# No Pool work in layer 0's projections, and the first 512 scales' weights between the two halves of the tokens

## The chip, the cores and the metric

The kernel runs on one core of a Trainium2 chip. The metric is the time of one execution on the device in microseconds (us), the median of three runs. In the profile the engines are PE (matrix products; PEld is its loading of weights), DVE (vector), ACT (scalar), POOL (general) and SP, which here only issues loads. ACT issues the stores of layer 0's projections.

## What is computed

Two layers of a diffusion backbone over 1024 tokens of 2048 channels in float32, with a context of 256 tokens. Layer 0 is attention, layer 1 a pooling layer. What matters here is how layer 0 begins: a modulation vector made from a conditioning vector scales and shifts the normed tokens, and the result is multiplied with a wide matrix.

```python
def _modulation(cvec, w, b):
    m = jax.nn.silu(cvec) @ w + b
    m = m[..., None, :]
    return m[..., :D_MODEL], m[..., D_MODEL:2 * D_MODEL], m[..., 2 * D_MODEL:]
...
    shift, scale, gate = _modulation(c, mod_w, mod_b)
    shift_c, scale_c, gate_c = _modulation(c_ctx, mod_w, mod_b)
    h = _rmsnorm(x, pre_g) * (1 + scale) + shift
    hc = _rmsnorm(ctx, pre_g) * (1 + scale_c) + shift_c

    proj = h @ w_in
    qA, qB = _split_q(proj[..., :Q_W])
    kA, vA, kB, vB = _split_kv(proj[..., Q_W:Q_W + KV_W])
    z = proj[..., Q_W + KV_W:]
...
    qA = _rope(_rmsnorm(qA, q_norm), cos, sin)
    kA = _rope(_rmsnorm(kA, k_norm), cos, sin)
```

Queries and keys get a rotary turn, the queries of 16 heads and the keys and values of 4 go to scratch in DRAM, and the gates `z` follow. Attention, the output projection and layer 1 come after that and are not touched.

## The kernel before

**Products.** Each float32 operand of a large product is cut into a high and a low part (`split`, line 144): ACT (or Pool) writes the rounded high part, DVE (or Pool) writes the source less the high part. A product is three passes, high by high, high by low, low by high. A 128x512 matmul is the unit of work of PE: three column blocks of 128, two halves of 512 tokens, 16 chunks of 128 rows and three passes make 288 of them. Weights come through tiles `wr` (two buffers) and are split into `wh` (ACT) and `wl` (DVE).

**Modulation.** `modulation(kind, j)` makes 512 channels of the scales (`kind` 1) or shifts (`kind` 0). It loads eight tiles `mraw` of 512 KB, two chunks of 128 rows each, through five buffers (`RAWS`), multiplies each of the 16 chunks by a column of the conditioning vector and adds the products up. `mod_add` (line 341) does a chunk on DVE (accumulator `mac`, line 355) or, for the chunks in `SHARED`, on ACT (`mpr`, line 349) and Pool (accumulator `max`, line 350). Of the scales' chunks Pool adds 9 of 16 (6 of the first 512 channels), of the shifts' 6. `mod_columns` (line 359) sums both accumulators over the partitions on PE (tile `mc`), and `mod_set` puts the result into `s0` or `b0`.

**The start.** `tokens(n)` loads a half of the tokens as four tiles `x` of 1 MB, takes their mean squares on ACT (line 396), and scales them on Pool and DVE in turn (line 398). `turned(n, ...)` transposes them on PE (`tx`, line 407), and ACT and DVE copy the result into `xT`.

**First two products.** `first` makes three blocks of queries with `hs`, which is `xT` times the scale without the shift (`scaled`: the high part on ACT, line 458, the low part on DVE, line 459). It goes by quarters of four chunks: quarter j needs `modulation(1, j)`. `second` makes three further blocks with the full `h` (`modulated`: `nw` on ACT, high part on Pool, low part on DVE); quarter j needs `modulation(0, j)`. What the missing shifts add to `first` is made later (`first_shifts`).

**The other blocks.** `step` makes two blocks at a time (192 matmuls) and then does some tasks of the rest of the modulation (`mod_rest`, all on DVE). Each query head's half goes through `q_out`: a copy `hc` and squares `sq` on ACT, the rotary turn (`rotated`: three operations on DVE into `ra` and `rt`, one buffer each, and a sum on Pool, line 537), a split into `hl` (high on ACT, low on Pool) and two stores. PE sums the squares over the partitions (`cs`, line 549).

**What sets the order.** A scheduler puts the instructions of each engine into one fixed order, and each engine runs its list strictly in that order. A load that waits for a free buffer holds up all later loads of the same queue.

```python
            if k in shared:
...
                    nc.scalar.activation(pr, w, AF.Copy, scale=c)
                    nc.gpsimd.tensor_tensor(accs[1], accs[1], pr, op=ALU.add)
...
                nc.vector.scalar_tensor_tensor(accs[0], w, c, accs[0], op0=ALU.mult, op1=ALU.add)
```

Of the kernel before, what the change touches and what calls it, by code (L numbers as in the profile page):

```python
# [17 lines left out]
P = 128  # L18
D = 2048
# [11 lines left out]
# A product of two float32 numbers, each cut exactly into two 12-bit parts.  # L31
PASSES = ((0, 0), (0, 1), (1, 0))
WT, WB, PB = 512, 4, 8
RAWS = 5
# [13 lines left out]
# Chunks of rows whose products ACT and Pool take, for shifts and scales.  # L48
SHARED = (1, 4, 7, 9, 12, 15), (1, 3, 5, 7, 9, 11, 13, 14, 15)


def _constants():
# [7 lines left out]
    # Blocks of keys before, at and after the queries' own; the context's are all open.  # L60
# [18 lines left out]
def tile_backbone(ctx, tc, ins, out):  # L79
# [4 lines left out]
    # Sums of the modulation over the rows, still to be added up over the partitions.  # L84
# [19 lines left out]
    # Which of four lots of partitions a partition belongs to.  # L104
# [24 lines left out]
    # Scratch in DRAM.  # L129
# [23 lines left out]
    def w_tiles(w, cols, kc=KC, hi="act", room=None):  # L153
        """Chunks of 128 rows of the weights w, in two parts: the first chunk, their number and the tiles."""
# [36 lines left out]
    def newton(r, v, t):  # L191
        """r = 1 / sqrt(v), with a Newton step; t is room for it."""
        nc.scalar.activation(r, v, AF.Sqrt)
        nc.vector.reciprocal(r, r)
        nc.vector.tensor_tensor(t, r, r, op=ALU.mult)
        nc.vector.tensor_tensor(t, t, v, op=ALU.mult)
        nc.vector.tensor_scalar(t, t, -0.5, 1.5, op0=ALU.mult, op1=ALU.add)
        nc.vector.tensor_tensor(r, r, t, op=ALU.mult)

    def rstd_rows(r, ss, tp, n, tag):  # L200
        """r = 1 / sqrt(ss / D + eps), elementwise."""
# [4 lines left out]
    def lots_of(d, a):  # L206
        """512 columns of d, as lots of 32 partitions with 128 columns of four of d's rows each."""
# [10 lines left out]
    # ---------------------------------------------------------------- attention weights  # L218
# [3 lines left out]
    # The pools of the units with an even number and, later, those with an odd one.  # L222
# [14 lines left out]
    def scores(u, kt, s_tile, c_tile, pinned=lambda i: i, pin=lambda i: i, band=None):  # L237
        """Attention weights of four heads' blocks of queries, with queries on the partitions."""
# [53 lines left out]
    # ---------------------------------------------------------------- layer 0: norms and projections  # L292
    with ExitStack() as st:
# [13 lines left out]
        # Small vectors, one column per 128 channels.  # L307
# [15 lines left out]
        # Scales and shifts of the attention layer's tokens, 512 channels at a time: products with the rows of the  # L323
        # weights, which the partitions add up first.
# [16 lines left out]
        def mod_add(accs, k, w, c, tp, shared):  # L341
            """Adds a chunk's products, on DVE or, the shared ones, on ACT and Pool."""
            if k in shared:
                if accs[1] is None:
                    accs[1] = tp.tile([P, 512], F32, tag="max", name="max", bufs=2)
                    nc.scalar.activation(accs[1], w, AF.Copy, scale=c)
                else:
                    pr = tp.tile([P, 512], F32, tag="mpr", name="mpr", bufs=2)
                    nc.scalar.activation(pr, w, AF.Copy, scale=c)
                    nc.gpsimd.tensor_tensor(accs[1], accs[1], pr, op=ALU.add)  # L350
            elif accs[0] is None:
                accs[0] = tp.tile([P, 512], F32, tag="mac", name="mac", bufs=2)[:, : w.shape[1]]
                nc.vector.tensor_scalar(accs[0], w, c, None, op0=ALU.mult)
            else:
                nc.vector.scalar_tensor_tensor(accs[0], w, c, accs[0], op0=ALU.mult, op1=ALU.add)  # L355

        def mod_columns(accs, n=4):
            """The sums over the partitions, a column per 128 channels."""
            t = mtile("mc")
            accs = [a for a in accs if a is not None]  # L360
            for i in range(n):
                for a in accs:
                    nc.tensor.matmul(t[:, i : i + 1], lhsT=a[:, i * P : (i + 1) * P], rhs=ones[:, 0:1], start=a is accs[0], stop=a is accs[-1])
# [13 lines left out]
        def modulation(kind, j, shared=None):  # L377
            accs = [None, None]
            for k, w in mod_rows("ev", kind, j, raws):
                mod_add(accs, k, w, csil[:, k, 0:1], p0, shared or SHARED[kind])  # L380
            with tc.high_priority(offset=AHEAD):
                mod_set(kind, j, 0, mod_columns(accs))

        # Tokens scaled by their root mean squares, then with channels on the partitions.
# [5 lines left out]
        def tokens(n):  # L390
            xt = []
            for t in range(4 * n, 4 * n + 4):
# [5 lines left out]
                (nc.vector if t % 2 else nc.gpsimd).tensor_scalar(a, a, rx[:, t : t + 1], 1.0, op0=ALU.mult, op1=ALU.mult)  # L398
# [18 lines left out]
        def project(c0, nm, beside=None):  # L417
            """Products of blocks c0.. of w_in's columns with the tokens, by (block, half), with others between them."""
# [15 lines left out]
        def three(c0):  # L434
            """Three blocks, by halves, and the weights' tiles, two chunks of rows at a time."""
# [743 lines left out]
```

## Time and profile before

| what | value |
|---|---|
| time, median of 3 runs | 3113.48 us (3112.36 to 3114.37) |
| the profiled execution | span 3115.6 us; no other time is recorded for it |
| PE busy | 2989.6 us, 96% |
| DVE busy | 1649.9 us, 53% |
| ACT busy | 1075.0 us, 35% |
| POOL busy | 424.1 us, 14% |
| mean granted clock of PE | 0.981 of full speed |

The busy shares are means over stages that differ. The start, `first` and `second` fill the first 239 us, the query steps go to about 560 us, gates, keys and values to about 1105 us, the last gates and attention to 1607 us, and the rest is the output projection and layer 1. A granted clock of 1.00 is PE's level of 2.4 GHz; at 0.5, 1.2 GHz, a matmul takes twice as long. A stretch with a clock of 0.87 is one in which PE ran part of the time at half speed.

### The profile page before, as it was taken

How to read it: one execution, taken by the hardware profiler on the slowest of the kernel's cores; microseconds unless marked ns; L12 is line 12 of the kernel's file. 1: busy time of each engine (PE TensorE's matmuls, PEld its weight loads, DVE VectorE, ACT ScalarE, POOL GpSimd, SP SyncE). 2: the span in 40 equal slices, each digit the busy share in tenths (PEclk: the TensorE clock that was granted, in tenths of full speed). 3: DMA queues.
4: the chain of work that ended last, by engine and by line, in shares of the span. 5: the costliest groups of instructions: out<-in, count | busy, mean ns of one | idle time of the engine just before them, and what ended most of it. 6: DMA issues, size and time to landing. Idle time of an engine off the chain costs nothing.

```text
span 3115.6 us, 38559 instructions
## 1 busy us (share of the span) xinstructions
PE 2989.6 (96%) x14102; PEld 2481.0 (80%) x14102; DVE 1649.9 (53%) x2725; ACT 1075.0 (35%) x2073; POOL 424.1 (14%) x327
## 2 busy tenths in 40 slices
PE   5899999899999999999899999999999999999998
PEld 5677777787888788888778888888888888888887
DVE  7968877555235748888753363623332323322434
ACT  6542312221111147776642352522222221222332
POOL 4643413000001100001220040300000001000000
PEclk8989999999999999999999999999999999999999
DMA  8738776888467854445555544423222121355734
GB/s 289 242 126 252 215 247 219 254 289 260 171 235 253 267 177 124 136 125 159 153 170 164 214 138 157 156 65 111 85 91 75 48 101 49 129 176 172 250 104 163
DMA packets 373011, 530.34 MB, mean 170 GB/s; under 512 B 28644, under 2 KB 215894, under 8 KB 371670
## 3 DMA queue, kind: packets, MB, share of 16 engines
q1 hardware_dynamic: 287990, 445.81, 44.7%
q10 hardware_dynamic: 84832, 82.07, 7.7%
q8 instruction: 111, 1.82, 0.2%
q14 instruction: 78, 0.64, 0.1%
HBM read 428.88 MB, written 98.91 MB: 169 GB/s over the span
## 4 chain that ended last, share of the span: by engine, by line
PE 70%; DMA 13%; DVE 9%; issue 3%; ACT 2%; POOL 2%; SPq 0%; ACTq 0%; DVEq 0%; POOLq 0%
PE g L186 32%; PE g L962 21%; DMA mraw<-in_od_mod_w_dram 5%; DVE mac L355 5%; PE o L904 4%; DMA mraw<-in_ev_mod_w_dram 3%; PE mx L186 3%; PE s L254 3%; PE t L850 3%; PE g L1043 2%; DVE wl L149 1%; DMA lsd<-ls 1%; DMA wr<-in_od_w_out_dram 1%; DMA rs<-lsd 1%; PE c L260 1%
## 5 line engine op out<-in xcount | busy, mean ns | idle before, releaser
L149 DVE TENSOR_TENSOR wl<-wr,wh 128x512 fp32r<-128x512 f32 (+1 forms) x576 | 414.9, 726 | 852.6 <-ACT wh L146 835.4
L186 PE MATMUL g<-h,wh 128*128 128x512 f32 x2368 | 756.8, 400 | 8.1 <-ACT fe L477 5.8
L146 ACT CAST wh<-wr 128x512 fp32r<-128x512 f32 (+1 forms) x576 | 349.6, 615 | 1100.2 <-PE g L186 563.5
L962 PE MATMUL g<-wh,a 128*128 128x512 f32 x1920 | 594.4, 390 | 0.1
L186 PE MATMUL g<-a,wh 128*128 128x512 f32 x1856 | 571.0, 389 | 0.0
L186 PEld LDWEIGHTS g<-h,wh 128*128 128x128 f32 x2368 | 453.9, 194 | 100.7 <-POOL h L148 5.9
L186 PE MATMUL g<-h,wl 128*128 128x512 f32 x1184 | 473.9, 401 | 14.2 <-DVE wl L149 14.1
L355 DVE SCALAR_TENSOR_TENSOR mac<-mraw,csil,mac 128x512 f32<-128x512 f32 x423 | 364.5, 862 | 120.2 <-DMA mraw<-in_od_mod_w_dram 64.8
L962 PEld LDWEIGHTS g<-wh,a 128*128 128x128 f32 x1920 | 360.1, 188 | 75.5 <-ACT wh L146 0.8
L186 PEld LDWEIGHTS g<-a,wh 128*128 128x128 f32 x1856 | 348.3, 188 | 72.4
L962 PE MATMUL g<-wl,a 128*128 128x512 f32 x960 | 373.7, 389 | 0.0
L186 PE MATMUL g<-a,wl 128*128 128x512 f32 x928 | 360.7, 389 | 0.0
L186 PEld LDWEIGHTS g<-h,wl 128*128 128x128 f32 x1184 | 227.9, 193 | 67.0 <-DVE wl L149 19.9
L962 PEld LDWEIGHTS g<-wl,a 128*128 128x128 f32 x960 | 180.2, 188 | 37.2
L186 PEld LDWEIGHTS g<-a,wl 128*128 128x128 f32 x928 | 174.2, 188 | 36.3
L149 DVE TENSOR_TENSOR tl<-t,th 128x512 fp32r<-128x512 f32 x236 | 160.0, 684 | 39.5 <-ACT th L146 38.0
L146 ACT CAST th<-t 128x512 fp32r<-128x512 f32 x236 | 135.9, 584 | 110.6 <-PE t L850 109.3
L904 PE MATMUL o<-th,vt 128*128 128x512 f32 x472 | 156.3, 412 | 2.5 <-ACT th L146 2.5
L850 PE MATMUL t<-ident,p 128*128 128x128 f32 x944 | 139.0, 276 | 10.5 <-DVE tl L149 10.1
L850 PEld LDWEIGHTS t<-ident,p 128*128 128x128 f32 x944 | 114.8, 142 | 38.2 <-DVE tl L149 15.5
L537 POOL TENSOR_TENSOR ra<-ra,rt 128x512 f32<-128x512 f32 x40 | 64.7, 1619 | 553.1 <-DMA mraw<-in_ev_mod_w_dram 287.8
L1106 POOL TENSOR_TENSOR s<-s 128x541 f32<-128x541 f32 (+1 forms) x32 | 38.1, 1190 | 587.4 <-DVE s L1106 561.7
(221 smaller groups left out, 3357.2 us busy)
## 6 DMA issues: line engine op xcount, KB each, us to landing
mraw<-in_ev_mod_w_dram SPq DMA_DIRECT2D x192, 256.0 KB, 4.0
mraw<-in_od_mod_w_dram SPq DMA_DIRECT2D x192, 256.0 KB, 4.6
wr<-in_od_w_in_dram SPq DMA_DIRECT2D x76, 512.0 KB, 3.6
wr<-in_ev_w_in_dram SPq DMA_DIRECT2D x68, 512.0 KB, 4.6
mraw<-in_ev_mod_w_dram SPq DMA_DIRECT2D x64, 512.0 KB, 5.2
wr<-in_ev_w_out_dram SPq DMA_DIRECT2D x64, 512.0 KB, 3.8
wr<-in_od_w_out_dram SPq DMA_DIRECT2D x64, 512.0 KB, 4.8
qd<-hl ACTq DMA_DIRECT2D x64, 256.0 KB, 2.9
```

What stands on the lines that cost most here:

```text
L146: nc.scalar.copy(dst_h, src)
L149: (lo or nc.vector).tensor_tensor(dst_l, src, f32(dst_h), op=ALU.subtract)
L186: pin(nc.tensor.matmul(o, lhsT=w[a][:, kk, m * P : (m + 1) * P], rhs=rhs(n, k, b), start=(k == 0 and i == 0), stop=(k == kc - 1 and i == 2),))
L254: pin(nc.tensor.matmul(s[:, sl], lhsT=qt[:, h, a], rhs=kt[:, b, sl], start=i == 0, stop=i == 2))
L260: pinned(nc.tensor.matmul(cs[:, hh], lhsT=qt[:, h + hh, a], rhs=kt[:, b, L:], start=i == 0, stop=i == 2))
L355: nc.vector.scalar_tensor_tensor(accs[0], w, c, accs[0], op0=ALU.mult, op1=ALU.add)
L537: nc.gpsimd.tensor_tensor(a, a, t, op=ALU.add)
L850: pin(nc.tensor.transpose(t[:, h * P : (h + 1) * P], ps[h][:, i * P : (i + 1) * P], ident))
L904: pin(nc.tensor.matmul(outs[u], lhsT=vt[:, a, kb], rhs=b, start=(i == 0 and jj == 0), stop=(last and jj == 2)))
L962: nc.tensor.matmul(o, lhsT=y[k][:, a, t * P : (t + 1) * P], rhs=wt[b][:, k - k0, :], start=(k == 0 and i == 0), stop=(k == KC - 1 and i == 2),
L1043: mm = nc.tensor.matmul(o, lhsT=w[a][:, k - k0, m * P : (m + 1) * P], rhs=hT[k][0][:, b], start=(k == 0 and i == 0), stop=(k == KC - 1 and ...
L1106: eng.tensor_tensor(nx[:, lo + d :], cur[:, lo + d :], cur[:, lo : W - d], op=ALU.add)
```

## The change

Pool is taken out of layer 0's projections, and the order of the start is changed:

- All 16 chunks of a modulation are multiplied and added on DVE; `SHARED`, `max` and `mpr` are gone, and `mod_columns` sums one accumulator.
- `mraw` has seven buffers in place of five.
- Every second tile `x` is scaled on ACT in place of Pool.
- The high part of `h`, and that of the context's tokens, is made on ACT in place of Pool.
- The sum of the rotary turn and the low part of `hl` (queries and keys) are made on DVE in place of Pool.
- The first half of the tokens is loaded and turned, then comes `modulation(1, 0)`, then the second half. Before, both halves came first.

Lines that were only comments are blank in the changed file, and its line numbers are up to ten lower.

```diff
-RAWS = 5
+RAWS = 7
...
-        def mod_add(accs, k, w, c, tp, shared):
-            """Adds a chunk's products, on DVE or, the shared ones, on ACT and Pool."""
-            if k in shared:
-                if accs[1] is None:
-                    accs[1] = tp.tile([P, 512], F32, tag="max", name="max", bufs=2)
-                    nc.scalar.activation(accs[1], w, AF.Copy, scale=c)
-                else:
-                    pr = tp.tile([P, 512], F32, tag="mpr", name="mpr", bufs=2)
-                    nc.scalar.activation(pr, w, AF.Copy, scale=c)
-                    nc.gpsimd.tensor_tensor(accs[1], accs[1], pr, op=ALU.add)
-            elif accs[0] is None:
-                accs[0] = tp.tile([P, 512], F32, tag="mac", name="mac", bufs=2)[:, : w.shape[1]]
-                nc.vector.tensor_scalar(accs[0], w, c, None, op0=ALU.mult)
+        def mod_add(a, k, w, c, tp):
+
+            if a is None:
+                a = tp.tile([P, 512], F32, tag="mac", name="mac", bufs=2)[:, : w.shape[1]]
+                nc.vector.tensor_scalar(a, w, c, None, op0=ALU.mult)
             else:
-                nc.vector.scalar_tensor_tensor(accs[0], w, c, accs[0], op0=ALU.mult, op1=ALU.add)
...
+                nc.vector.scalar_tensor_tensor(a, w, c, a, op0=ALU.mult, op1=ALU.add)
+            return a
...
-                (nc.vector if t % 2 else nc.gpsimd).tensor_scalar(a, a, rx[:, t : t + 1], 1.0, op0=ALU.mult, op1=ALU.mult)
+                if t % 2:
+                    nc.vector.tensor_scalar(a, a, rx[:, t : t + 1], 1.0, op0=ALU.mult, op1=ALU.mult)
+                else:
+                    nc.scalar.activation(a, a, AF.Copy, scale=rx[:, t : t + 1])
...
-        x_halves = [tokens(n) for n in range(NH)]
-        for n in range(NH):
-            turned(n, x_halves[n])
-        modulation(1, 0, (1, 3, 5, 7, 9, 11))
+
+        turned(0, tokens(0))
+        modulation(1, 0)
+        turned(1, tokens(1))
...
-                    split(hT[k][n][:, 0], hT[k][n][:, 1], w, "pool")
+                    split(hT[k][n][:, 0], hT[k][n][:, 1], w)
...
-            nc.gpsimd.tensor_tensor(a, a, t, op=ALU.add)
+            nc.vector.tensor_tensor(a, a, t, op=ALU.add)
...
-            split(o[:, 0, :w], o[:, 1, :w], src, lo=nc.gpsimd)
+            split(o[:, 0, :w], o[:, 1, :w], src)
...
-                split(o[:, 0], o[:, 1], w, "pool")
+                split(o[:, 0], o[:, 1], w)
...
-            split(o[:, 0], o[:, 1], r, lo=nc.gpsimd)
+            split(o[:, 0], o[:, 1], r)
```

In the fences that follow a row is a line of code, an operation with output and inputs, the tile's shape, and how often the row repeats. The first place is SP's queue of loads at the start of the program; `vr` are small vectors. Before:

```order
L313 DMA vr<-in_ev_mod_b_dram 32x128
L394 DMA x<-in_x_dram 128x2048 x8
L330 DMA mraw<-in_ev_mod_w_dram 128x2x512 x5
L162 DMA wr<-in_ev_w_in_dram 128x2x384 x2
L313 DMA vr<-in_od_pre_g_dram 16x128
L313 DMA vr<-in_od_pool_scale_dram 16x128
```

In the changed program the same place reads:

```order
L311 DMA vr<-in_ev_mod_b_dram 32x128
L383 DMA x<-in_x_dram 128x2048 x4
L328 DMA mraw<-in_ev_mod_w_dram 128x2x512 x7
L383 DMA x<-in_x_dram 128x2048 x4
L160 DMA wr<-in_ev_w_in_dram 128x2x384 x2
L311 DMA vr<-in_od_pre_g_dram 16x128
```

Seven tiles of the first modulation moved in front of the second half of the tokens; its eighth stays behind that half and the first two tiles of `w_in`.

The second place is DVE's list where `scaled` makes the first low parts `hs`; `s_75` are the scales, and a row with `mac` is a chunk of a modulation. Before:

```order
L353 TENSOR_SCALAR mac<-mraw,csil 128x512
L355 SCALAR_TENSOR_TENSOR mac<-mraw,csil,mac 128x512 x4
L369 TENSOR_TENSOR s_75<-mc,v_70 128x4
L370 SCALAR_TENSOR_TENSOR s_75<-s_75,v_70 128x4
L355 SCALAR_TENSOR_TENSOR mac<-mraw,csil,mac 128x512
L459 SCALAR_TENSOR_TENSOR hs<-xT,s_75,hs 128x512 x2
L355 SCALAR_TENSOR_TENSOR mac<-mraw,csil,mac 128x512
L459 SCALAR_TENSOR_TENSOR hs<-xT,s_75,hs 128x512 x3
```

In the changed program the last rows before the first `hs`, and `hs` itself, read:

```order
L345 SCALAR_TENSOR_TENSOR mac<-mraw,csil,mac 128x512 x2
L403 COPY xT<-tx 128x4x128
L345 SCALAR_TENSOR_TENSOR mac<-mraw,csil,mac 128x512
L403 COPY xT<-tx 128x4x128
L345 SCALAR_TENSOR_TENSOR mac<-mraw,csil,mac 128x512
L403 COPY xT<-tx 128x4x128
L343 TENSOR_SCALAR mac<-mraw,csil 128x512
L345 SCALAR_TENSOR_TENSOR mac<-mraw,csil,mac 128x512
L450 SCALAR_TENSOR_TENSOR hs<-xT,s_75,hs 128x512 x2
```

The last copies of the second half's `xT`, 11 of the 15 additions of the second modulation and the first operation of the third now stand in front of the first `hs`.

The third place is DVE's list in the query steps, where the heads 0 to 7 end; `hc` is a head's copy, `rope_t` the tables of the turn, `v_71` the gain. Before:

```order
L536 SCALAR_TENSOR_TENSOR ra<-hc,v_71,rope_t 128x512
L669 COPY rq<-cs 128x4
L536 SCALAR_TENSOR_TENSOR rt<-hc,v_71,rope_t 64x512 x2
L536 SCALAR_TENSOR_TENSOR ra<-hc,v_71,rope_t 128x512
L536 SCALAR_TENSOR_TENSOR rt<-hc,v_71,rope_t 64x512 x2
L669 COPY rq<-cs 128x4
L536 SCALAR_TENSOR_TENSOR ra<-hc,v_71,rope_t 128x512
L149 TENSOR_TENSOR wl<-wr,wh 128x512 x2
```

In the changed program:

```order
L527 SCALAR_TENSOR_TENSOR ra<-hc,v_71,rope_t 128x512
L528 TENSOR_TENSOR ra<-ra,rt 128x512
L527 SCALAR_TENSOR_TENSOR rt<-hc,v_71,rope_t 64x512 x2
L660 COPY rq<-cs 128x4
L147 TENSOR_TENSOR hl<-ra,hl 128x512
L147 TENSOR_TENSOR wl<-wr,wh 128x512
L527 SCALAR_TENSOR_TENSOR ra<-hc,v_71,rope_t 128x512
```

The sum `ra` and the low part `hl`, two operations for each half of a head, came into DVE's list, with the next half's `rt` between them. From the first attention units on, the lists of all engines read the same in both programs.

## Rows read from the trace of the kernel before

**Rows 1.** The page: its span, and the chain that ended last, by engine.

```profile
span 3115.6 us, 38559 instructions
...
PE 70%; DMA 13%; DVE 9%; issue 3%; ACT 2%; POOL 2%; SPq 0%; ACTq 0%; DVEq 0%; POOLq 0%
```

**Rows 2.** Windows: stretch, its length, each engine's busy time, clock, DMA share, GB/s.

```profile
0.00:57.70 57.70, 25.48 (x145) 23.69 (x145) 39.45 (x96) 35.87 (x59) 18.26 (x15) 0.84 0.85 306
...
57.70:190.00 132.30, 112.19 (x470) 90.83 (x470) 125.85 (x134) 74.68 (x121) 85.15 (x58) 0.87 0.71 236
190.00:239.30 49.30, 49.30 (x222) 40.75 (x220) 20.59 (x29) 17.64 (x28) 13.97 (x16) 0.97 0.26 90
...
239.30:368.30 129.00, 117.34 (x549) 96.10 (x548) 116.69 (x148) 38.43 (x67) 56.63 (x36) 0.95 0.71 215
368.30:560.00 191.70, 183.11 (x804) 151.11 (x804) 148.88 (x208) 40.52 (x75) 45.06 (x28) 0.96 0.76 240
560.00:1105.00 545.00, 521.52 (x2488) 435.21 (x2489) 274.41 (x393) 101.96 (x194) 36.42 (x28) 0.98 0.75 248
```

**Rows 3.** Waits of PE, 57.7 to 239.3 us: total us, times, longest.

```profile
PE g L186 <- DVE wl L149: 7.5, 4, 3.7
PE g L186 <- ACT fe L477: 5.8, 1, 5.8
```

**Rows 4.** Timeline of PE where `first` begins, `second` begins, and `second` has ended.

```profile
57.71 2.08 PE L186 MATMUL g<-hs,wh 128*128 128x512 f32 x4 [1.20 <-ACT hs L458]
...
152.46 1.19 PE L186 MATMUL g<-h,wh 128*128 128x512 f32 x2 [5.82 <-ACT fe L477]
...
239.34 0.38 PE L509 MATMUL st<-sink_r,ones 1*128 1x8 f32 x2
```

**Rows 5.** Timeline of DVE, 126 to 137 us: start, length, instruction.

```profile
126.26 0.75 DVE L355 SCALAR_TENSOR_TENSOR mac<-mraw,csil,mac 128x512 f32<-128x512 f32 x1
126.92 0.75 DVE L459 SCALAR_TENSOR_TENSOR hs<-xT,s,hs 128x512 fp32r<-128x512 f32 x1
127.58 0.48 DVE L353 TENSOR_SCALAR mac<-mraw,csil 128x512 f32<-128x512 f32 x1
127.98 1.41 DVE L459 SCALAR_TENSOR_TENSOR hs<-xT,s,hs 128x512 fp32r<-128x512 f32 x2
...
133.28 0.55 DVE L149 TENSOR_TENSOR wl<-wr,wh 128x384 fp32r<-128x384 f32 x1
133.75 1.78 DVE L459 SCALAR_TENSOR_TENSOR hs<-xT,s,hs 128x512 fp32r<-128x512 f32 x1
135.45 1.77 DVE L355 SCALAR_TENSOR_TENSOR mac<-mraw,csil,mac 128x512 f32<-128x512 f32 x1
```

**Rows 6.** Timeline of POOL, 118 to 140 us.

```profile
118.72 1.28 POOL L350 TENSOR_TENSOR max<-max,mpr 128x512 f32<-128x512 f32 x1 [0.89 <-ACT mpr L349]
...
131.00 8.94 POOL L350 TENSOR_TENSOR max<-max,mpr 128x512 f32<-128x512 f32 x4 [7.85 <-ACT mpr L349]
```

**Rows 7.** Groups of DVE by form, 0 to 239.3 us: busy us, mean ns, idle before.

```profile
L355 DVE SCALAR_TENSOR_TENSOR mac<-mraw,csil,mac 128x512 f32<-128x512 f32 x63 | 67.4, 1071 | 1.7 <-DMA mraw<-in_ev_mod_w_dram 1.2
...
L459 DVE SCALAR_TENSOR_TENSOR hs<-xT,s,hs 128x512 fp32r<-128x512 f32 x32 | 31.0, 1004 | 1.8 <-ACT hs L458 1.8
L149 DVE TENSOR_TENSOR wl<-wr,wh 128x384 fp32r<-128x384 f32 x32 | 29.9, 948 | 5.5 <-ACT wh L146 5.3
```

**Rows 8.** The chain in a stretch of layer 1: start, length, piece.

```profile
2308.74 43.53 PE g L186 x192
```

**Rows 9.** Groups of ACT by form, 0 to 239.3 us.

```profile
L396 ACT ACTIVATE junk<-x 128x2048 bf16<-128x2048 f32 x8 | 15.3, 1908 | 2.7 <-DMA x<-in_x_dram 2.7
```

**Rows 10.** Groups of POOL by form, 0 to 239.3 us.

```profile
L350 POOL TENSOR_TENSOR max<-max,mpr 128x512 f32<-128x512 f32 x49 | 79.7, 1629 | 48.8 <-ACT mpr L349 46.7
```

**Rows 11.** Waits of PE, 239.3 to 368.3 us.

```profile
PE cs L549 <- ACT sq L668: 9.7, 7, 2.9
```

**Rows 12.** Waits of DVE, 229 to 560 us.

```profile
DVE mac L355 <- DMA mraw<-in_ev_mod_w_dram: 20.8, 26, 3.2
```

More of the change, by code (lines that the diff above doesn't have):

```diff
@@ L339, in mod_rows, with mod_columns @@
             return rows_of(ins[layer + "_mod_w"][0][:, base : base + 512], raws, pinned)
-        def mod_add(accs, k, w, c, tp, shared):
-            if k in shared:
-                if accs[1] is None:
-                    accs[1] = tp.tile([P, 512], F32, tag="max", name="max", bufs=2)
-                    nc.scalar.activation(accs[1], w, AF.Copy, scale=c)
-                else:
-                    pr = tp.tile([P, 512], F32, tag="mpr", name="mpr", bufs=2)
-                    nc.scalar.activation(pr, w, AF.Copy, scale=c)
-                    nc.gpsimd.tensor_tensor(accs[1], accs[1], pr, op=ALU.add)
-            elif accs[0] is None:
-                accs[0] = tp.tile([P, 512], F32, tag="mac", name="mac", bufs=2)[:, : w.shape[1]]
-                nc.vector.tensor_scalar(accs[0], w, c, None, op0=ALU.mult)
-            else:
-                nc.vector.scalar_tensor_tensor(accs[0], w, c, accs[0], op0=ALU.mult, op1=ALU.add)
-        def mod_columns(accs, n=4):
+        def mod_add(a, k, w, c, tp):
+            if a is None:
+                a = tp.tile([P, 512], F32, tag="mac", name="mac", bufs=2)[:, : w.shape[1]]
+                nc.vector.tensor_scalar(a, w, c, None, op0=ALU.mult)
+            else:
+                nc.vector.scalar_tensor_tensor(a, w, c, a, op0=ALU.mult, op1=ALU.add)
+            return a
+        def mod_columns(a, n=4):
             t = mtile("mc")
-            accs = [a for a in accs if a is not None]
             for i in range(n):
-                for a in accs:
-                    nc.tensor.matmul(t[:, i : i + 1], lhsT=a[:, i * P : (i + 1) * P], rhs=ones[:, 0:1], start=a is accs[0], stop=a is accs[-1])
+                nc.tensor.matmul(t[:, i : i + 1], lhsT=a[:, i * P : (i + 1) * P], rhs=ones[:, 0:1], start=True, stop=True)
             return t[:, :n]
@@ L375, in raws, with modulation @@
             return p0.tile([P, 2, 512], F32, tag="mraw", name="mraw", bufs=RAWS)
-        def modulation(kind, j, shared=None):
-            accs = [None, None]
+        def modulation(kind, j):
+            a = None
             for k, w in mod_rows("ev", kind, j, raws):
-                mod_add(accs, k, w, csil[:, k, 0:1], p0, shared or SHARED[kind])
+                a = mod_add(a, k, w, csil[:, k, 0:1], p0)
             with tc.high_priority(offset=AHEAD):
-                mod_set(kind, j, 0, mod_columns(accs))
+                mod_set(kind, j, 0, mod_columns(a))
         xT = [actx.tile([P, 4, NH, HL], F32, tag="a", name="xT") for _ in range(4)]
@@ L633, in mod_rest @@
         def mod_rest(layer, kind, j, i=0):
-            a = [None, None]
+            a = None
             for k, w in mod_rows(layer, kind, j, rest_raws, True):
-                mod_add(a, k, w, csil[:, k, i : i + 1], ev, ())
+                a = mod_add(a, k, w, csil[:, k, i : i + 1], ev)
             if layer == "ev" and kind < 2:
-                unfinished.append(lambda: mod_set(kind, j, i, mod_columns([a[0]])))
+                unfinished.append(lambda: mod_set(kind, j, i, mod_columns(a)))
             else:
                 d = dram([P, 512], f"md{len(later)}")
-                store(d, a[0])
+                store(d, a)
                 later.append(d)
         def first_shifts():
-            a = [None, None]
+            a = None
             for k, w in rows_of(w_in[:, : 3 * P], rest_raws):
-                mod_add(a, k, w, b0[:, k, 0:1], ev, ())
-            unfinished.append(lambda: nc.vector.tensor_copy(fb, mod_columns(a[:1], 3)))
+                a = mod_add(a, k, w, b0[:, k, 0:1], ev)
+            unfinished.append(lambda: nc.vector.tensor_copy(fb, mod_columns(a, 3)))
         def mod_end():
```

1 line of the change is left out of this document (removed).

## The prediction

> **What bounds the kernel now.** I began with the page: of the chain that ended last 70% is PE and 9% DVE [rows 1], so a change that touches DVE, ACT and Pool pays only where PE waits for them. Since the instruction lists are the same in both programs from attention on, only the stretch up to 1105 us can move, and the windows cut it up [rows 2]. From 560 to 1105 us PE is busy for 521.5 of 545.0 us, from 368.3 to 560 for 183.1 of 191.7: little to win. From 190.0 to 239.3 PE is busy for all 49.30 us. But from 57.7 to 190.0, where `first` and the larger part of `second` run, PE works 112.2 of 132.3 us at a clock of 0.87 and DVE 125.9, or 95%. There DVE sets the pace. The timeline puts the beginning of `first` at 57.71, of `second` at 152.46 and the end of `second` at 239.34 [rows 4]; together they take 181.6 us for 576 matmuls. Where PE waits for nothing, 192 matmuls take 43.53 us, 0.2267 us each [rows 8], so 576 need 130.6 us. The difference, 51 us, is what this change can work on here. The waits say little of it (7.5 us for `wl`, 5.8 for `fe`) [rows 3], since most gaps stand behind short waits for `hs` and `h` and in half-speed matmuls after them; the window shows it better than the list of waits.
>
> Why DVE is full is in two timelines. With Pool idle, a chunk's multiply-add takes 0.75 us and the next starts 0.66 us later; from 131.00 to 139.9, while Pool adds four times without a pause, the same operation takes 1.77 and the next starts 1.70 us later [rows 5, 6]. Over the first 239 us the 63 multiply-adds have a mean of 1.071, the 32 `hs` 1.004, the 32 `wl` 0.948 us, against 0.75 (0.745 unrounded) and 0.55 quiet [rows 5, 7]. Pool thus costs DVE 63 × 0.326 + 32 × 0.259 + 32 × 0.398 = 20.5 + 8.3 + 12.7 = 41 us in these three groups. The Trainium skill, SBUF — State Buffer, section Who interferes with whom, says that a DVE instruction with two SBUF inputs contends with a GpSimd instruction that reads SBUF, and that the loser blocks for the whole instruction. The trace agrees in kind: 1.02 us more, beside 1.28 for a quiet Pool addition. By that rule alone the bound of what DVE gets back up to 239 us would be all of Pool's busy time, 18.3 + 85.2 + 14.0 = 117 us, where the rows give 41.
>
> **The change up to the end of `second`.** DVE takes over 57 chunks (6 + 3 × 9 of the scales, 4 × 6 of the shifts). I price by distance from start to start: 0.67 us for an operation with two inputs, 0.40 for a chunk's first, 0.47 for `wl` [rows 5]. The 57 come to 38 us, which is just about the 41 that go. On balance DVE's total hardly changes; what changes is where it lies. A quarter of `first` now holds 16 chunks (15 × 0.67 + 0.40 = 10.45), eight `hs` (5.3), four `wl` (1.9) and small ones (0.4): 18.1 us, against 72 × 0.2267 + 0.6 for `mc` = 16.9 us of PE. DVE and PE come near to balance.
>
> The first `hs` gets later. Fifteen more chunks stand ahead of it (27 + 2 of 48, where 14 stood), 9.8 us. DVE is idle for 57.7 − 39.45 = 18.2 us before it [rows 2], which could hide all (57.7) or none; the latter, with today's list ahead of it at 36.5 us by the same prices, is 36.5 + 9.8 + 18.2 = 64.5. The loads speak for the later side: eight tiles `x` of 1 MB, 17 `mraw` of 0.5 and some `wr` are 18.5 MB, at 306 GB/s [rows 2] 60.5 us. I take 62.5, a loss of 4.8. This order pays later: most of the second modulation is then done.
>
> From there to the shifts of the third quarter of `second` DVE has 83 chunks (54.5 us), 32 `hs` (21.4), 16 low parts of `h` (10.7) and about 45 `wl` (21): 108 us, at today's 95% 114, so 176.5; I add 3.6 for the five short dependent operations from the last chunk to the first `h` (0.7 each). Then PE has two quarters left: 180 + 33.8 = 214. PE by itself needs 62.5 + 8 × 16.9 + 5.8 for the turn from `first` to `second` [rows 3] + some 5 for half-speed matmuls, 208.5. The later, 214, holds: **239.3 − 214 = 25 us gained**.
>
> ACT takes four scalings of `x` and 40 high parts, and loses the 57 products `mpr`. No scaling of 128x2048 on ACT is in the trace; it lies between 0 and 1.91, that of `junk` with the same shape [rows 9], and I take the latter, 7.6 us in all. Four of them were Pool's, and ACT is busy for 23.7 of the first 57.7 us and 74.7 of the next 132.3 [rows 2], so they are hidden; without that cover the start is 7.6 later. Pool's end as such frees nothing: of its 49 additions' idle time 46.7 us is for ACT's `mpr` [rows 10].
>
> The loads must keep up. Up to the shifts of the third quarter 42.9 MB are loaded, 17.7 of them by 57.7 us (57.7 × 306). The other 25.2 at today's 236 GB/s [rows 2] take 107 us, to 164, before the 176 above. Loads bind below 25.2 MB / 118 us = 213 GB/s, a margin of only a tenth, and two more `mraw` buffers widen it.
>
> **The query steps, 239.3 to 368.3 us.** Sixteen halves of heads bring some 32 operations to DVE, 32 × 0.67 = 21 us. DVE is busy for 116.7 us there, Pool for 56.6 [rows 2]; with the ratio of rows 7 (0.745 / 1.071 = 0.70) DVE's present list is 82 quiet, so 103 to 110 after. PE's matmuls need some 103. Now the stretch takes 129.0, and PE waits 9.7 us in `cs` for ACT's squares [rows 11], which stand in turn behind the chain through `ra` and `hl`, with Pool's two long operations in it. If the larger of the lists set the pace, −19 (or to −26 for PE's alone); if the waits for `hl` and `mraw` merely change place, 0. I take **−11**, the `cs` wait and a little of the clock of 0.95. The stretches after it: 0, with ±4 each, since PE is near its full share.
>
> **Sum.** 25 + 11 = 36 us: the profiled span of 3115.6 becomes 3079.6. The span lies 2.1 above the median of the runs, so 3113.5 − 36 = 3077 us.
>
> **Rivals.** A change of less than 0.2%, 6.2 us, can't be told from none; that is my bound throughout.
>
> R1, the forecast: 3077, own range 3062 to 3092 (the start 57.7 to 64.5, the query steps −19 to 0, the two later stretches). Chance 0.66.
>
> R2, loads are late. SP's queue is strict: a `wr` that waits for a buffer holds up the `mraw` behind it, and seven `mraw` are ahead of the second half of `x`. DVE then waits where Pool once shared the work. With 190 GB/s the 25.2 MB take 133 us, 15 more than 118, of which `mraw`'s extra buffers hide a little: 13 us less gain, 3090. For it: the margin above. Against it: DVE's multiply-adds waited only 1.2 us for `mraw` in 239 us [rows 7]. Chance 0.15.
>
> R3, the query steps give back. `ra`'s sum and `hl`'s low part now stand in one list with `mod_rest`, whose chunks wait for loads; DVE waited 20.8 us for `mraw` in 26 places [rows 12]. A chunk that waits holds the sum behind it, then `hl`, then the next half's squares' buffers and PE's `cs`. If 13 of these 20.8 come through to PE: −25 + 13 = −12, 3101. Pool's list had no such chunks. Chance 0.12.
>
> R4, slower. DVE's operations stay as long as they are now, because something other than Pool (ACT's larger share, the loads) lengthens them. Then 57 × 1.07 = 61 us land on an engine that is 95% busy; less the 15 us by which DVE now is ahead of need at 190.0 (PE, busy throughout from there, would need the third quarter's shifts at 239.3 − 33.8 = 205), +46: about 3160. It decides from a spacing of some 0.9 us on, a third above the quiet one, where 57 operations and the longer rest eat the 25 us. Against it: 0.75 and 1.77 stand within one `first`, under the same loads, and Pool is what differs [rows 5, 6]. Chance 0.07. The Trainium skill, Perfetto Trace Analysis, section Optimizing Scalar/DVE Operations, speaks against the change: where DVE is saturated, it says, moving work to ScalarE or even GPSIMD may make sense, with the reserve that the shared port may undo it. No row before shows which of the two wins in the sum; R4 is what it would be if the first did.
>
> **How the numbers follow.** The likeliest is 3077. R1's range holds about four fifths of R1 and part of R2's; up to 3102 it takes in R2 and R3, and below 3062 the query steps at −19 with a start at 57.7 end at about 3060. So 3060 to 3102, with R4 and the tails outside. Faster by over 6.2 us: R1, R2 and most of R3, 0.88; within: 0.05, R3 with more than 13 given back; slower: 0.07, R4.
>
> **What would show it.** Right: no multiply-add or `hs` of 1.7 us up to 239, means at 0.75 and 0.55; POOL idle up to attention; `first` beginning at about 62 and `second` ending at about 214, with a clock over 0.9 between. Wrong: means above 0.9 (R4); DVE idle for `mraw` in `first` and `second` (R2); the boundary now at 368.3 reached less than 12 us earlier, with PE's `cs` waits grown (R3). What I trust least is the balance of 18.1 to 16.9 us in a quarter: if DVE and PE hand over in small pieces, each wait for `h` can drop PE to half speed again, and `second` ends nearer 225 than 214.

## The result, and the profile after

| what | before | after |
|---|---|---|
| time, median of 4 runs | 3113.22 us (3112.36 to 3114.37) | 3047.00 us (3042.50 to 3049.37) |
| ratio to before, 95% interval | | 0.9782 (0.9768 to 0.9796) |
| span of the profiled execution | 3115.6 us | 3040.8 us |
| DVE busy | 1649.9 us | 1612.4 us |
| POOL busy | 424.1 us | 169.3 us |

The change made the kernel 66 us faster, 2.2%. That is in the direction of the forecast, but below the range: 3077 was predicted, 3060 to 3102 given. The profiled execution after is the one of 3042.5 us, the fastest of the four, so differences of spans are larger (74.8 us) than the difference of medians (66.2). What follows about places in time goes by the spans, and some 8 us of that gain are scatter between executions.

The page of the changed kernel, its span and its chain by engine, answers to [rows 1]:

```profile
span 3040.8 us, 38187 instructions
...
PE 80%; DMA 11%; DVE 5%; issue 2%; ACT 1%; POOL 0%; SPq 0%; ACTq 0%; DVEq 0%; POOLq 0%
```

PE's share of the chain rose from 70 to 80%, and DVE's and Pool's fell from 11 to 5%: the program is nearer to being one long list of matmuls.

The windows show where the time went if they are cut at the same points of both programs: the first product with `hs`, the end of `second` (576 products done), the second of the two `mc` after some 980 products (980 before, 991 after; 11 products are 2.5 us), the last `mc` of the query steps, and the first scores of attention. The columns are those of [rows 2]: stretch, length, busy time of PE, PEld, DVE, ACT and POOL, clock, DMA share, GB/s. The kernel before, cut so:

```profile
57.70:239.34 181.64, 161.53 (x690) 131.58 (x690) 146.48 (x163) 92.36 (x149) 99.12 (x74) 0.90 0.59 196
239.34:368.36 129.02, 117.31 (x550) 96.10 (x549) 116.67 (x149) 38.39 (x67) 56.68 (x37) 0.95 0.71 215
368.36:557.79 189.43, 182.16 (x797) 150.24 (x797) 148.85 (x207) 38.98 (x73) 45.01 (x28) 0.96 0.76 240
557.79:1109.66 551.87, 527.13 (x2517) 439.93 (x2516) 275.80 (x395) 104.76 (x199) 36.42 (x28) 0.98 0.75 248
1109.66:3115.60 2005.94, 1976.03 (x9409) 1639.43 (x9407) 922.68 (x1717) 764.65 (x1530) 168.61 (x146) 1.00 0.42 133
```

The changed kernel:

```profile
0.00:56.90 56.90, 23.20 (x137) 21.98 (x137) 39.45 (x108) 37.53 (x54) 0.20 (x4) 0.85 0.93 347
56.90:208.85 151.95, 145.11 (x635) 117.86 (x636) 132.54 (x221) 80.82 (x139) 0.00 (x0) 0.97 0.69 231
208.85:319.61 110.76, 110.76 (x558) 93.79 (x557) 105.34 (x181) 37.43 (x66) 0.00 (x0) 1.00 0.81 247
319.61:495.96 176.35, 174.52 (x787) 144.80 (x785) 139.55 (x227) 39.44 (x72) 0.00 (x0) 0.99 0.81 256
495.96:1035.45 539.49, 522.00 (x2517) 438.45 (x2516) 271.66 (x415) 107.67 (x204) 0.00 (x0) 0.98 0.76 252
1035.45:3040.80 2005.35, 1975.99 (x9409) 1639.54 (x9407) 923.86 (x1717) 764.11 (x1530) 169.11 (x146) 1.00 0.42 133
```

Read the lengths in pairs. The start got 0.8 us shorter (57.70 to 56.90, which is within the scatter of the runs below), `first` and `second` 29.7 us, the two query steps after them 18.3, the other query steps 13.1 (20.8 and 10.6, if the 11 products are counted where they stood), gates, keys and values 12.4, and the remaining 2005 us are the same to 0.6. From the end of `second` to the third row PE is now busy for all of 110.76 us at a clock of 1.00. DVE has more operations than before in each of the first five stretches (221 for 163 in the second row), and in all of these but the first less busy time (132.5 for 146.5 in the second).

The groups of DVE by form, 0 to 200.6 us of the changed kernel, say why. They answer to [rows 7]:

```profile
L345 DVE SCALAR_TENSOR_TENSOR mac<-mraw,csil,mac 128x512 f32<-128x512 f32 x120 | 87.4, 745 | 0.8
L450 DVE SCALAR_TENSOR_TENSOR hs<-xT,s,hs 128x512 fp32r<-128x512 f32 x32 | 22.7, 743 | 0.0
L147 DVE TENSOR_TENSOR h<-nw,h 128x512 fp32r<-128x512 f32 x32 | 21.1, 685 | 2.7 <-ACT h L144 2.7
L147 DVE TENSOR_TENSOR wl<-wr,wh 128x384 fp32r<-128x384 f32 x32 | 17.7, 553 | 7.5 <-ACT wh L144 7.3
```

The 120 multiply-adds have the quiet length, 0.745 us against a mean of 1.071 before; twice as many cost 20 us more than the 63 did. The low parts `h` had been lengthened as well, a fourth group beside the three that the prediction priced, and the shorter ones give back 32 × 0.329 = 10.5 us. In the kernel before, 0 to 239.3 us, their row is:

```profile
L149 DVE TENSOR_TENSOR h<-nw,h 128x512 fp32r<-128x512 f32 x32 | 31.4, 1014 | 6.8 <-POOL h L148 6.8
```

### The profile page after: what moved, and what is told of

It is laid out like the page before. It is cut to its first block, busy times and chain, and to the rows that moved or that the text cites. A ratio compares the mean times of both kernels' runs of the same rounds, so it can differ in the third digit from the quotient of the medians.

```text
span 3040.8 us, 38187 instructions
## 1 busy us (share of the span) xinstructions
PE 2951.6 (97%) x14038; PEld 2456.4 (81%) x14038; DVE 1612.4 (53%) x2866; ACT 1067.0 (35%) x2060; POOL 169.3 (6%) x150
## 4 chain that ended last, share of the span: by engine, by line
PE 80%; DMA 11%; DVE 5%; issue 2%; ACT 1%; POOL 0%; SPq 0%; ACTq 0%; DVEq 0%; POOLq 0%
PE g L184 41%; PE g L953 21%; DMA mraw<-in_od_mod_w_dram 5%; PE o L895 4%; PE mx L184 3%; PE s L252 3%; PE t L841 3%; DVE mac L345 2%; PE g L1034 2%; DMA mraw<-in_ev_mod_w_dram 2%; DMA lsd<-ls 1%; DMA rs<-lsd 1%; DMA wr<-in_od_w_out_dram 1%; PE c L258 1%; DMA zt<-in_ctx_dram 1%
## 5 line engine op out<-in xcount | busy, mean ns | idle before, releaser
L147 DVE TENSOR_TENSOR wl<-wr,wh 128x512 fp32r<-128x512 f32 (+1 forms) x576 | 395.8, 692 | 843.2 <-ACT wh L144 831.1
L184 PE MATMUL g<-h,wh 128*128 128x512 f32 x2368 | 743.0, 394 | 1.9 <-ACT h L144 1.8
L184 PEld LDWEIGHTS g<-h,wh 128*128 128x128 f32 x2368 | 445.3, 190 | 93.6 <-ACT h L144 2.5
L184 PE MATMUL g<-h,wl 128*128 128x512 f32 x1184 | 465.0, 393 | 5.0 <-DVE wl L147 5.0
L345 DVE SCALAR_TENSOR_TENSOR mac<-mraw,csil,mac 128x512 f32<-128x512 f32 x480 | 357.1, 748 | 112.6 <-DMA mraw<-in_od_mod_w_dram 61.1
L857 POOL TENSOR_TENSOR zt<-zt,rs 128x512 f32<-128x512 f32 x32 | 49.6, 1552 | 1426.0 <-DMA zt<-zd 1075.5
L252 PE MATMUL s<-kt,qt 128*128 128x512 f32 x384 | 103.4, 404 | 0.0
```

Source lines behind the costliest of these rows:

```text
L147: (lo or nc.vector).tensor_tensor(dst_l, src, f32(dst_h), op=ALU.subtract)
L184: pin(nc.tensor.matmul(o, lhsT=w[a][:, kk, m * P : (m + 1) * P], rhs=rhs(n, k, b), start=(k == 0 and i == 0), stop=(k == kc - 1 and i == 2),))
L252: pin(nc.tensor.matmul(s[:, sl], lhsT=qt[:, h, a], rhs=kt[:, b, sl], start=i == 0, stop=i == 2))
L345: nc.vector.scalar_tensor_tensor(a, w, c, a, op0=ALU.mult, op1=ALU.add)
L857: GATE.tensor_tensor(zt, zt, rs.rearrange("p q h -> p h q"), op=ALU.mult)
```

## The experiments

Twelve kernels were run, each a small edit of the changed kernel, with ratios to the kernel before that were measured on the same chip. The changed kernel has 0.9782; a difference of 0.001 is 3.1 us, and differences under some 0.002 are within the intervals. A place that is the same in all is the `mc` of the first blocks' shifts, after 768 products, here called the common `mc`: at 258.05 us in the changed kernel, at 296.14 before.

**One edit undone at a time.** The order of the start:

```diff
-        turned(0, tokens(0))
-        modulation(1, 0)
-        turned(1, tokens(1))
+        x_halves = [tokens(n) for n in range(NH)]
+        for n in range(NH):
+            turned(n, x_halves[n])
+        modulation(1, 0)
```

> The changed kernel (3047) with only the order of the start undone: both halves of the tokens are loaded and turned, then the first scales are made. Theory (Pool's operations lengthened DVE's, the order matters little): first begins 4 to 8 us later than at 56.9, the multiply-adds stay at 0.75 us, and the time is 3050 to 3056. Rival (the order of the start brought much of what was gained up to the end of second): half of those 30 us or more come back, 3062 or more.

Measured: 3051.88 us, ratio 0.9795 (0.9781 to 0.9810). The time is in the theory's range, but not for its reason: `first` begins at 57.95, 1.0 us later and not 4 to 8, and runs with the changed kernel's own start begin it at 57.3 to 58.2. The common `mc` comes at 262.94, 4.9 later, most of it after `second` begins (138.38 against 137.66), and the multiply-adds stay at 745 ns. The order is worth some 4 us by the ratios, which the intervals don't tell from nothing.

The sum of the turn and the low part of `hl` back on Pool:

```diff
-            nc.vector.tensor_tensor(a, a, t, op=ALU.add)
+            nc.gpsimd.tensor_tensor(a, a, t, op=ALU.add)
...
-            split(o[:, 0, :w], o[:, 1, :w], src)
+            split(o[:, 0, :w], o[:, 1, :w], src, lo=nc.gpsimd)
...
-            split(o[:, 0], o[:, 1], r)
+            split(o[:, 0], o[:, 1], r, lo=nc.gpsimd)
```

> The changed kernel with only the sum of the rotary turn and the low part of hl back on Pool. Theory (in the query steps too, Pool's operations lengthen DVE's and hold up the chain that ends in cs): second ends at about 209 as in the changed kernel, and the gain from there on, some 44 us in the profiled executions, is lost: 3080 to 3091. Rival (the later gain follows from the earlier one, because the steps start with work done ahead): 3047 to 3060.

Measured: 3077.84 us, 0.9875 (0.9854 to 0.9895), 29 us slower by the ratios, just below the theory's 3080. The first `cs` stands at 209.28 (208.85 in the changed kernel), so nothing is lost up to there; then `mc` comes at 333.86 (319.61), 521.54 (495.96), and attention begins at 1069.7 (1035.45): the loss is 14, 11 and 9 us in the three stretches that gained 18, 13 and 12. The rival is out. DVE's groups by form from 209 to 521.6 us, and PE's waits from 209 to 521, show both a lengthening and waits in the chain; `rt` had 748 and 686 ns, the multiply-adds 749, in the changed kernel:

```profile
L345 DVE SCALAR_TENSOR_TENSOR mac<-mraw,csil,mac 128x512 f32<-128x512 f32 x135 | 115.8, 858 | 28.9 <-DMA mraw<-in_ev_mod_w_dram 23.0 <-DMA mraw<-in_od_mod_w_dram 3.4
...
L527 DVE SCALAR_TENSOR_TENSOR rt<-hc,v,rope_t 64x512 f32<-64x512 f32 x29 | 33.0, 1136 | 4.7 <-POOL ra L528 4.2
L524 DVE TENSOR_TENSOR rt<-hc,rope_t 64x512 f32<-64x512 f32 x32 | 31.1, 971 | 6.0 <-POOL ra L528 5.6
```

```profile
PE cs L540 <- ACT sq L659: 8.5, 4, 2.6
PE mc L352 <- DVE mac L345: 5.3, 1, 5.3
```

The modulation's shared chunks back on ACT and Pool:

```diff
-RAWS = 7
+RAWS = 5
...
-                a = mod_add(a, k, w, csil[:, k, 0:1], p0)
+                c = csil[:, k, 0:1]
+                if k not in (shared or SHARED[kind]):
+                    a = mod_add(a, k, w, c, p0)
+                elif x is None:
+                    x = p0.tile([P, 512], F32, tag="max", name="max", bufs=2)
+                    nc.scalar.activation(x, w, AF.Copy, scale=c)
+                else:
+                    pr = p0.tile([P, 512], F32, tag="mpr", name="mpr", bufs=2)
+                    nc.scalar.activation(pr, w, AF.Copy, scale=c)
+                    nc.gpsimd.tensor_tensor(x, x, pr, op=ALU.add)
...
```

> The changed kernel with only the modulation's shared chunks back on ACT and Pool, in the new order of the start, and with five mraw buffers in place of seven, since their tiles need the room (five buffers alone are a run of their own). Theory (contention): the multiply-adds that remain on DVE rise to about 1.0 us again, second ends at 225 to 235 in place of 209, 3062 to 3075. Rival (order of the start): 3047 to 3055. Rival (Pool's share was a help where DVE is full, and the gain came from the other edits): 3040 or less.

Measured: 3073.03 us, 0.9864 (0.9845 to 0.9883), 25.5 us slower. `first` begins at 62.38, the common `mc` comes at 283.82 in place of 258.05. DVE's groups from 0 to 210 us are back near their lengths of before:

```profile
L345 DVE SCALAR_TENSOR_TENSOR mac<-mraw,csil,mac 128x512 f32<-128x512 f32 x63 | 64.7, 1028 | 5.1 <-DMA mraw<-in_ev_mod_w_dram 4.7
L465 DVE SCALAR_TENSOR_TENSOR hs<-xT,s,hs 128x512 fp32r<-128x512 f32 x32 | 34.5, 1096 | 1.8 <-ACT hs L464 1.8
```

The high part of `h`, and that of the context, back on Pool, and, as the control of the run before, five `mraw` buffers:

```diff
-                    split(hT[k][n][:, 0], hT[k][n][:, 1], w)
+                    split(hT[k][n][:, 0], hT[k][n][:, 1], w, "pool")
...
-                split(o[:, 0], o[:, 1], w)
+                split(o[:, 0], o[:, 1], w, "pool")
```

> The changed kernel with only the high part of h (and of the context's) back on Pool. Theory: 32 operations of Pool lie in the stretch from 132 to 200 us, where DVE has slack behind the chunks but the low part of h has to wait for Pool; second ends 5 to 12 us later, 3050 to 3060. Rival (the high part was the larger share of the gain): 3065 or more.

```diff
-RAWS = 7
+RAWS = 5
```

> The changed kernel with five mraw buffers in place of seven. Theory (the loads have room): 3047 to 3053. Rival (the loads are near the bound, and the two more buffers carry them over waits of the queue): DVE waits 10 us or more for mraw up to the end of second, 3057 or more.

Measured: 3052.74 us, 0.9802 (0.9787 to 0.9817) for the high part, 6 us, which the intervals don't tell from nothing, with the low parts `h` at 833 and the multiply-adds at 783 ns; 3047.91 us, 0.9782 (0.9766 to 0.9798) for five buffers, nothing. The four undone parts (0.0013, 0.0093, 0.0082, 0.0020) sum to 0.0208, against 0.0218 of the whole, each with an interval of some ±0.002. Nothing large is left over; the scaling of `x` on ACT was not undone by itself.

**Pool's work by itself.** In the runs above Pool's work and what DVE no longer has to do change together. So in the next three Pool got useless work in the changed kernel, on about as many chunks as it once shared (60 for 57; Pool's additions had been 49 [rows 10], since ACT alone made the first shared chunk of each modulation), and DVE kept its own:

```diff
                 a = mod_add(a, k, w, csil[:, k, 0:1], p0)
+                if k in IDLE[kind]:
+                    nc.gpsimd.tensor_tensor(w, w, w, op=ALU.add)
...
+        IDLE = (1, 4, 7, 9, 12, 15), (1, 3, 5, 7, 9, 11, 13, 14, 15)
```

> The changed kernel, and beside it Pool adds each of 60 mraw chunks to itself (128x512, two inputs) after DVE has used it; nothing needs the result, and the buffer comes free later. Theory (Pool's reads lengthen DVE's operations with two inputs): DVE's multiply-adds, hs and wl have means of 0.9 to 1.1 us in the stretch up to the end of second, which ends 30 to 55 us later than at 209: 3077 to 3100. Rival (Pool cost time only where something waited for its results): DVE's lengths stay at 0.75, 3047 to 3055.

```diff
-                    nc.gpsimd.tensor_tensor(w, w, w, op=ALU.add)
+                    nc.gpsimd.memset(w, 0.0)
```

> As the run before, but Pool clears the chunk (a memset, which reads nothing) in place of adding it to itself; the same waits and the same buffers. Theory (it is Pool's reading that lengthens DVE's operations): lengths stay at 0.75 us, 3047 to 3055. Rival (any work of Pool, or the later release of the mraw buffers, costs the time): as the run before, 3077 or more.

```diff
-                    nc.gpsimd.memset(w, 0.0)
+                    for _ in range(3):
+                        nc.gpsimd.memset(w, 0.0)
```

> The run with Pool's writes on the 60 chunks, with three memsets for each chunk in place of one, so that Pool is busy for some 99 us in the first 210 us, about as long as with the additions (90). Theory (Pool's reading): DVE's multiply-adds stay at 0.75 us, 3042 to 3055. Rival (the length of Pool's work or the mraw buffers that it holds, of which the single memsets took only a third): 3065 or more.

Measured: with additions 3085.42 us, 0.9901 (0.9881 to 0.9921), 37 us slower, and the common `mc` at 299.06, 41 us late; with one memset 3043.89 us, 0.9769 (0.9753 to 0.9786); with three 3047.96 us, 0.9791 (0.9775 to 0.9807). The groups by form with the additions, up to 250 us, where `second` has ended:

```profile
L345 DVE SCALAR_TENSOR_TENSOR mac<-mraw,csil,mac 128x512 f32<-128x512 f32 x120 | 114.3, 968 | 0.9
...
L371 POOL TENSOR_TENSOR mraw<-mraw 128x512 f32<-128x512 f32 x60 | 90.0, 1506 | 123.6 <-DVE mac L345 61.6 <-issue 26.2 <-DVE nxv L201 19.6
```

The same with three memsets, up to 210 us:

```profile
L372 POOL MEMSET mraw<- 128x512 f32 x180 | 93.5, 540 | 85.8 <-DVE mac L345 60.7 <-DVE nxv L201 19.8
...
L345 DVE SCALAR_TENSOR_TENSOR mac<-mraw,csil,mac 128x512 f32<-128x512 f32 x120 | 87.6, 746 | 0.8
```

Pool is busy for 90 and for 93.5 us, and holds the same buffers after the same instruction. With reads the multiply-adds go to 968 ns, with writes they stay at 746. What costs the time is Pool's reading beside DVE. Its being busy and its holding the buffers account for little: with three memsets the common `mc` comes at 264.50, 6.4 us late in place of 41, and the time of the whole is within the intervals.

The same in the query steps, to part the lengthening from the wait for Pool's results, with no result of Pool's in the chain:

```diff
             nc.vector.tensor_tensor(a, a, t, op=ALU.add)
+            nc.gpsimd.tensor_tensor(t, t, t, op=ALU.add)
...
             split(o[:, 0], o[:, 1], r)
+            nc.gpsimd.tensor_tensor(r, r, r, op=ALU.add)
```

> The changed kernel; after the turn's sum Pool adds rt to itself, and after the split of hl it adds ra to itself. Nothing needs the results, but both tiles have one buffer, so that the next half's turn waits for Pool to be done with them. All arithmetic that is needed stays on DVE. Theory (the 31 us that the turn on Pool cost are the lengthening of DVE's operations by Pool's reads): 3070 to 3090. Rival (they are the wait for Pool's results in the chain to cs): 3055 or less.

```diff
-            nc.gpsimd.tensor_tensor(t, t, t, op=ALU.add)
+            for _ in range(3):
+                nc.gpsimd.memset(t, 0.0)
...
-            nc.gpsimd.tensor_tensor(r, r, r, op=ALU.add)
+            for _ in range(3):
+                nc.gpsimd.memset(r, 0.0)
```

> As the run before, with three memsets (0.55 us each, about the 1.6 us of one addition) in place of each addition, so that Pool is busy for as long and holds rt and ra for as long, but reads nothing. Theory (Pool's reading): 3045 to 3055. Rival (holding the buffers, or any work of Pool): as the run before, 3065 or more.

Measured: 3065.11 us, 0.9848 (0.9825 to 0.9872), 20.5 us slower, for the reads, between the theory's 3070 and the rival's 3055; 3041.78 us, 0.9775 (0.9760 to 0.9791), for the writes. Two rows from 209 to 510 us, with the reads:

```profile
L345 DVE SCALAR_TENSOR_TENSOR mac<-mraw,csil,mac 128x512 f32<-128x512 f32 x124 | 105.2, 849 | 13.9 <-DMA mraw<-in_ev_mod_w_dram 11.7 <-DMA mraw<-in_od_mod_w_dram 0.5
...
L527 DVE SCALAR_TENSOR_TENSOR rt<-hc,v,rope_t 64x512 f32<-64x512 f32 x30 | 31.3, 1045 | 0.7
```

The lengths come near those of the kernel with the turn on Pool (858 and 1136). From the end of `second`, product 576, to product 1728, where the query steps end, the changed kernel takes 287.5 us, the run with the turn on Pool 316.9, the one with reads 316.0 and the one with writes 288.4. In the query steps the reads alone thus cost about as much as the turn on Pool, and little is left for the chain through Pool's results; PE waits for `sq` before `cs` here too, 5.4 us in place of 8.5. That the whole loses 20.5 us in place of 29 doesn't speak for the chain: this edit leaves out the keys' low parts, so that after the query steps Pool is busy for 11.3 us in place of 30.4 up to the first scores, and the way from product 1728 to them takes 537.7 us in place of 542.7. The rest of the difference lies outside these stretches.

**Two attempts to go on.** All tiles `x` scaled on DVE:

```diff
-                if t % 2:
-                    nc.vector.tensor_scalar(a, a, rx[:, t : t + 1], 1.0, op0=ALU.mult, op1=ALU.mult)
-                else:
-                    nc.scalar.activation(a, a, AF.Copy, scale=rx[:, t : t + 1])
+                nc.vector.tensor_scalar(a, a, rx[:, t : t + 1], 1.0, op0=ALU.mult, op1=ALU.mult)
```

> The changed kernel with all eight tiles x scaled on DVE and none on ACT. In the changed kernel PE waits 26 us for ACT's scalings at the start. Theory (the loads set the start, DMA share 0.93): within 3 us of the changed kernel, 3044 to 3050. Rival (ACT's mean squares and scalings in turn set it): first begins 3 to 6 us earlier, 3041 to 3044.

Measured: 3050.65 us, 0.9789 (0.9774 to 0.9804). `first` begins 1.4 us earlier, at 55.47, but `second` 5.4 us later, at 143.04. No gain; the theory's 3050 is just about met, the rival's early start is not. DVE is busy for 76.9 of the 80.8 us of `first` in the changed kernel; that its further work makes `second` late is argued, not shown.

The gates of the attention on DVE as well:

```diff
-        GATE = nc.gpsimd
+        GATE = nc.vector
```

> The changed kernel with the gates of the attention (32 products zt, 1.55 us each on Pool) on DVE as well. Theory (Pool's reads cost time only where DVE's operations have two inputs in SBUF and DVE sets the pace; in attention the low parts tl come from PE's results, have a mean of 0.685 us beside Pool, and DVE is 74% busy): within 5 us of the changed kernel, 3042 to 3052. Rival (Pool's work costs DVE time in every stage): 10 us or more are gained, 3037 or less.

Measured: 3138.78 us, 1.0082 (1.0064 to 1.0099): 93 us slower than the changed kernel, which neither side expected. The waits of DVE and PE from 1025 to 1640 us in this run:

```profile
DVE zt L857 <- DMA rs<-lsd: 78.9, 29, 4.8
...
PE t L841 <- DVE tl L147: 38.5, 16, 3.6
PE o L895 <- DVE tl L147: 38.2, 20, 5.0
```

The gate's factor `rs` comes back through DRAM, and the multiplication waits for its load. In the changed kernel Pool had this wait, 163.0 us in 20 places, and DVE waited 20.8 us for what came of it. On DVE the low parts `tl` stand behind it, PE waits for them 76.7 us in place of 16.0, and its clock falls to 0.95 from 0.99 (1040 to 1600 us). The low parts themselves have 685 ns with Pool at the gates and without; in the changed kernel the 50 that run while Pool is busy have 683 ns, the other 186 have 686. One of their inputs is PE's result, and Pool doesn't lengthen them.

## Why the prediction was right about the mechanism and too small

**The lengthening (right).** The quiet prices held: multiply-adds at 0.745, `hs` at 0.743 and `wl` at 0.553 us, and no operation of 1.7 us. R4 is refuted. "On balance DVE's total hardly changes" did not hold: up to the end of `second` it fell from 185.9 to 172.0 us with 57 chunks more, since the low parts `h` gave back 10.5 us beyond the 41. Of the advice and the reserve in the Trainium skill, Perfetto Trace Analysis, section Optimizing Scalar/DVE Operations, the reserve about the shared port decided here. The Trainium skill, SBUF — State Buffer, section Who interferes with whom, also says that a GpSimd instruction that only writes doesn't contend; the runs with memsets agree (746 ns). A full block of the loser isn't what the sums show. Before, 117 us of Pool's work lengthened the three groups by 41 us, with `h` and the chunks' first multiplications (784 for 477 ns) by some 54. And 90 us of additions lengthened the multiply-adds by 120 × 0.223 = 27 us, and `hs` and `wl` (means of 836 and 735 ns up to 250 us) by 3.0 and 5.8, with `h` (735 ns) some 37.

**`first` and `second` (right).** From the first product to the end of `second` the forecast had 214 − 62.5 = 151.5 us; it took 151.95. The clock in it was 0.97, and PE's waits for DVE and ACT come to 7.6 us. The balance in a quarter, which I trusted least, held in the sum alone: the quarters of `first` took 22.4, 20.3, 17.8 and 20.3 us, against the 18.1 of DVE's list.

**The start (too late by 5.6 us).** The step was "18.5 MB, at 306 GB/s 60.5 us". The loads ran at 347 GB/s (DMA share 0.93 for 0.85), so 306 was no bound of the loads. SP's queue waited 12.8 us in this stretch for multiply-adds to release `mraw` before, and 6.3 us now; but the run with five buffers begins `first` at 57.53, and that the releases made the difference isn't shown. The run with the old order gives 57.95, so the new order is not the main reason. ACT's scalings of `x` took 2.0 us each, a little over the 1.91 that I took for the upper bound, and cost at most the 1.4 us by which the run with all on DVE began earlier.

**The two query steps after `second` (too small by 7.3 us).** I took −11 from bounds of 0 and −26; it was −18.3. PE's `cs` waits are gone, and the clock rose from 0.95 to 1.00. The "larger of the lists", −19, was the right reading, but the list was PE's: busy for all of 110.76 us, 108.3 without the 11 products, where I had 103, beside DVE's 105.3.

**The later stretches: the step that failed.** "The stretches after it: 0, with ±4 each, since PE is near its full share" was measured at −13.1 and −12.4 us (−10.6 and −12.4 by products), 23 to 25 of the 39 us by which the span's gain of 74.8 exceeded the 36 forecast. A busy share of 95% at a clock of 0.96 was no full share: a matmul at half speed (0.425 us from one to the next, from 59.59 to 61.29 us before, against 0.227) is counted as busy for twice as long. From 368.36 to 557.79 PE was idle for 7.3 us and is now for 1.8, which gives 5.4; the other 7.6 us came out of busy time itself (182.16 to 174.52 us), 2.5 by the 11 products and the rest as the clock went from 0.96 to 0.99. From product 980 to the first scores, which is both stretches, the kernel before took 740.4 us and the changed one 718.3; the eight runs whose edits leave these stretches alone took 720.6 to 724.8, so that the gain is rather 16 to 22 us than 25. With the turn on Pool it is 735.0, with the high part, in which the context's falls here, 728.4. Most of the gain thus belongs to the two operations of the turn that I had priced for the stretch before and not carried on into these two, although Pool's 45.0 and 36.4 busy microseconds stood in [rows 2]; what the context's high part adds, one execution doesn't settle.

**R2 and R3.** Neither came. With five buffers in place of seven the time is the same, so loads had room. DVE still waits for `mraw`, but PE doesn't wait for what stands behind. From 209 to 496 us the longest of DVE's waits, answering to [rows 12], and the only one of PE's are:

```profile
DVE mac L345 <- DMA mraw<-in_ev_mod_w_dram: 21.6, 22, 2.4
...
PE mc L352 <- DVE mac L345: 1.8, 1, 1.8
```

## What to carry to other kernels

Price a helper engine by what it does to the lengths of its neighbour's operations, not by its own list: compare the same form beside it and without it, and do so in every stage where it runs. A stage in which PE is 95% busy at a clock of 0.96 still lost 6 to 7% of its time to waits and what follows from them. And before moving an operation onto a busy engine, look at what it waits for: computing is cheap there, but waiting for a load through DRAM holds up everything behind it.

## What the runs showed of the hardware

A reading addition on Pool and a DVE operation with two inputs in SBUF lengthen each other. Of the 63 multiply-adds before, the 35 that ran while Pool was busy took 1.33 us on average, the other 28 took 0.745; Pool's addition went from 1.28 us [rows 6] to a mean of 1.63 [rows 10]. Over a stage that is some 0.4 to 0.5 us of DVE for each microsecond of Pool (54 for 117, 37 for 90). Memsets of the same total length leave the multiply-adds at 746 ns. Of DVE's operations with one input, a chunk's first multiplication was lengthened too: in the kernel before it took 0.48 us by itself and 1.48 us at 49.95, beside an addition of Pool from 49.72 to 51.15:

```profile
49.95 1.48 DVE L353 TENSOR_SCALAR mac<-mraw,csil 128x512 f32<-128x512 f32 x1
```

```profile
49.72 1.43 POOL L350 TENSOR_TENSOR max<-max,mpr 128x512 f32<-128x512 f32 x1 [7.28 <-ACT mpr L349]
```

One operation with one input was longer beside memsets as well: in the run with three of them a scaling of `x` on DVE (128x2048) took 1.54 us at 50.12, where Pool cleared tiles from 47.82 to 52.13, and 1.28 us by itself.
